# Attention's value products: one-pass products on the whole array in place of 64-column fp32 pairs

## The chip, the cores and the metric

The program runs on one core of one Trainium2 chip. A core has a matrix engine (TensorE, PE in the profile; its weight loads are PEld), an elementwise engine (VectorE, DVE), an engine for functions and copies (ScalarE, ACT), a general one (GpSimd, POOL) and an engine that issues transfers (SyncE, SP). TensorE writes to PSUM, which has eight banks of 128 partitions by 512 fp32 numbers; the others compute from there or from SBUF. The metric is the device time of one execution in microseconds. Before the change the median of three runs is 1974.89 us (1970.23 to 1979.09).

## The reference

Two layers of a block that mixes three token mixers over 1024 latent tokens (a grid of 16 rows and 64 columns) and 256 context tokens, width 1024, all in fp32. The input projection feeds neighbourhood attention (8 heads of 64), an mLSTM in two directions, and a Hyena long convolution; their gated outputs are concatenated, projected and added to the input. The part that matters here is the attention: a latent query sees keys in a window of 8 rows and 16 columns around it, with a bias by relative position, and all 256 context keys:

```python
s = jnp.concatenate([s_lat.reshape(s_lat.shape[:4] + (kr * NA_KBLK,)), s_ctx], axis=-1)
p = jax.nn.softmax(s, axis=-1).astype(v.dtype)
p_lat = p[..., :kr * NA_KBLK].reshape(s_lat.shape)
p_ctx = p[..., kr * NA_KBLK:]
o = jnp.einsum('bhjqic,bijchd->bjqhd', p_lat, vw) + jnp.einsum('bhjqn,bnhd->bjqhd', p_ctx, vc)
```

In the first layer the context tokens attend too, to the context alone. The last line, probabilities times values, is what the change rewrites.

## The kernel before

**Streams and the order of TensorE's work.** The kernel is written as Python generators, called streams, that emit instructions. TensorE's instructions run in the order in which they are emitted. Before TensorE work a stream yields what it needs (tiles, a free PSUM bank, or a name that another stream announces), and `flow` (line 196) picks the stream of the best rank whose needs are met by an estimated clock (`Clock`, line 48). That clock counts a TensorE product by `mm` (line 179), 70 ns and 1/960 us per element for a VectorE instruction, 80 ns and 1/1200 us for a ScalarE one (`RATE`, line 50), places each in its engine's first gap, and adds a margin of 0.3 us. Attention's units have rank 1, the preparation of keys and values 0.9, the input projections 2: projections fill what attention leaves. The order on the other engines is not written out by hand.

**Precision.** Two kinds of product occur. Where both operands are fp32, TensorE takes four passes over the columns, and a product leaves two rows in the trace. Where the operands are of the type `F32R`, it takes one pass and leaves one row; such an operand is split into a high part (rounded to that type) and a low part (what is left of the fp32 number), and products of the parts are summed. The projections and the scores are made so already: three products for a projection, two for the scores.

**Attention** (`na`, line 1246). For each layer and head, `keys` (line 1256) loads and splits queries and keys, and `values` (line 1280) loads the values of the context and of four column blocks, transposes them (tile `avt`) and copies them, tokens on partitions, to `aVn`, with 64 columns for the head. Four streams `work` (line 1311) take the units in turn: a unit is a head and a block of 16 grid columns, 256 queries in two halves of 128 (or, in layer 0, the 256 context queries). There are 40 units in layer 0 and 32 in layer 1. A unit

- makes the scores in PSUM (`apl` for the window, `apc` for the context), adds the bias on VectorE with the maximum, takes exponentials on ScalarE, and scales each row on GpSimd or VectorE (tile `ae`);
- then goes through up to three groups (line 1380): transposes the blocks of a group on TensorE into one of two `tp` banks (`apt`), copies them to SBUF (`ph`, ScalarE for groups 0 and 2, VectorE for group 1, line 1390), and in the next round multiplies them with the values (`apo`, line 1412). Groups 0 and 1 have 4 blocks, so two products of 256 columns, group 2 has 2 blocks, so two products of 128 columns; a context unit has group 0 alone;
- adds the two halves of the one output bank (`o`): ScalarE copies one half (`at`), VectorE adds the other (`ay`, line 1424), and the bank is free for the next unit.

The two products of a group have 64 columns of weights each, and go to the two halves of the array:

```python
for i, (t, s, os) in enumerate(groups[gi - 1][1]):
    self.mm(po[HP[i], os], lhsT=v[:, t, :], rhs=x[:, s], start=gi == 1, stop=gi == ng, beside=i > 0)
```

So the upper 64 rows of the output hold one key tile's part and the lower 64 the other's, and their sum is the result. Units keep their order by announced names (`pv`): the transposes of a unit's first group wait for the second group's products of the unit before, and its own first products for the last of that unit. `out_early` (line 1452) can start the output projection while heads are left, if the input projections are through by then.

Of the kernel before, what the change touches and what calls it, by code (L numbers as in the profile page):

```python
# [13 lines left out]
F32 = mybir.dt.float32  # L14
F32R = mybir.dt.float32r
BF16 = mybir.dt.bfloat16
ACTF = mybir.ActivationFunctionType
ALU = mybir.AluOpType
AX = mybir.AxisListType
PSUM = bass.MemoryType.PSUM  # L20
DRAM = bass.MemoryType.DRAM

DM = 1024          # model width
L, LC = 1024, 256  # latent and context tokens
LT = L + LC
NH = 256           # hyena channels
GW = 64            # grid width
# [3 lines left out]
NCH = LT // 128    # mLSTM chunks; 8 and 9 are the context  # L31

# column blocks of w_in, 128 columns each, in the order of the host layout
# [4 lines left out]
GM = 34            # the 16 gate columns, kept apart  # L38
# [3 lines left out]
RAWX, RAWC, RAWN = 1, 1027, 1284   # padded layout of the inputs of the short convolutions  # L42
UC = 1026                          # where the context starts in their outputs

BANKS = dict(pj=2, s=3, tp=2, o=1)  # uses of the PSUM banks


class Clock:
    """An estimate of when the emitted instructions run; the order of the tensor engine's follows it."""
    RATE = dict(vector=(0.07, 1 / 960), scalar=(0.08, 1 / 1200), gpsimd=(0.2, 1 / 480))   # us per instruction, per element  # L50
# [6 lines left out]
    def region(ap):  # L57
        """(tensor, rows, columns) that hold what an access pattern covers."""
# [13 lines left out]
    def ready(self, aps):  # L72
        """When all that is in aps is there."""
# [8 lines left out]
    def slot(self, ap):  # L82
        """When the memory of a tile is free of what was there before."""
# [15 lines left out]
    def vacant(self, key, bufs):  # L99
        """When the first of the memories of a kind is free."""  # L100
        taken = self.slots.get(key, [])
        return 0.0 if len(taken) < bufs else min(self.used.get(n, 0.0) for n in taken)

    def run(self, engine, us, after):
        """Put an instruction in the engine's first gap."""
# [40 lines left out]
class Timed:  # L146
    """An engine whose instructions the clock notes."""
# [13 lines left out]
class Kern:  # L161
    def __init__(self, tc, I, out, depth=2):
# [4 lines left out]
        self.fb = dict(o="o", s="s", tp="tp")     # banks of the filters  # L167
        self.known, self.streams, self.bankkey = set(), [], {}

    # ------------------------------------------------------------------ order of the tensor engine's work  # L170
    # Streams are generators that emit instructions. Before work of the tensor engine they yield what it needs, a
    # tuple of access patterns, or a time, or the name of something that another stream announces (a set: the first of them). The tensor
    # engine issues in the order of emission; of the streams that are ready by the clock, the first goes next.
# [5 lines left out]
    def mm(self, o, lhsT, rhs, start, stop, beside=False):  # L179
        """A matrix product; beside: on columns of the array next to those of the one before, at the same time."""  # L180
# [39 lines left out]
    # ------------------------------------------------------------------ set-up  # L220
# [19 lines left out]
    def want(self, tag, *aps, extra=0.0):  # L240
        """Wait until aps are there and a bank is free."""
# [8 lines left out]
    # columns of per-channel parameters: cols[:, l, ...]  # L250
# [4 lines left out]
    def small(self):  # L255
        """Small things that are needed all along."""
# [6 lines left out]
    # ------------------------------------------------------------------ adaLN  # L263
# [11 lines left out]
    def ada_mod(self, l, pool, ahead):  # L275
        """Shift and scale of a layer as columns."""
# [19 lines left out]
    def ada_cols(self, l, m, ks):  # L296
        """Columns ks of shift and scale from m, whose rows 32 q, 32 q + 1 hold the q-th quarter of them."""
# [17 lines left out]
    def ada_late(self, pool):  # L315
        """What is left of adaLN: the layers' gates and the second's shift and scale, in passing."""
# [4 lines left out]
        for j, (l, part, kt) in enumerate(todo):  # L321
# [26 lines left out]
            # the gate times the gain of the layer's last norm, as rows in DRAM  # L348
# [1642 lines left out]
```

## Time and profile before

| | |
|---|---|
| median of three runs | 1974.89 us |
| span of the profiled execution | 1971.5 us, 28340 instructions |
| TensorE busy | 1859.0 us (94%), 10008 products and transposes |
| VectorE busy | 1063.8 us (54%) |
| ScalarE busy | 787.1 us (40%) |
| GpSimd busy | 460.1 us (23%) |
| transfers | 328.91 MB, two hardware queues |

No other time of the profiled execution is recorded than its span; it lies 3.4 us below the median. A row of the profile names the line, engine and operation, the tiles (output, then inputs), and shapes as partitions by elements. Almost all instructions are emitted through helpers, so their line is that of a helper (L182 products, L186 transposes, L155 the rest) and the tiles tell them apart. Ends of TensorE's instructions are modelled and overlap the next one's start; the distance between starts is what an instruction costs the queue.

### The profile page before, as it was taken

To read this page: it belongs to the slowest core of one execution; us is meant where nothing else is said; L and a number is where in the kernel's file an instruction comes from. 1 tells how busy PE (TensorE), PEld (TensorE's weight loads), DVE (VectorE), ACT (ScalarE), POOL (GpSimd) and SP (SyncE) were. 2 spreads that over 40 slices of the span, in tenths; PEclk is the share of its full clock that TensorE was granted. 3 is DMA by queue.
4 is the path that set the end of the run, shared out by engine and by line. 5 is a ranking of instruction groups with operands and counts; after the bars stand their busy time and mean duration, and the time that the engine had idled before them with its cause. 6 is when DMAs were issued, how large, how long until landed. Compare 5 with 4: busy or idle time off the path is not lost. (4 is left out here: it accounts for less than half of the span.)

```text
span 1971.5 us, 28340 instructions
## 1 busy us (share of the span) xinstructions
PE 1859.0 (94%) x10008; PEld 1410.4 (72%) x10008; DVE 1063.8 (54%) x2398; ACT 787.1 (40%) x1545; POOL 460.1 (23%) x368
## 2 busy tenths in 40 slices
PE   8699989998999899999999999999799989999998
PEld 2365867787787776676777876778687867676776
DVE  3744444537736466676545544434753476666533
ACT  3645342414423255444434434322323255454321
POOL 1534111323220121121222123222412112122300
PEclk9799999999999999999999999999999999999999
DMA  8476887863221657666354348764221455454533
GB/s 316 140 239 212 284 232 241 235 229 104 81 82 46 180 146 224 194 212 216 105 192 139 139 146 234 224 196 162 80 96 65 141 150 160 129 157 134 180 128 107
DMA packets 233610, 328.91 MB, mean 167 GB/s; under 512 B 22509, under 2 KB 162185, under 8 KB 231550
## 3 DMA queue, kind: packets, MB, share of 16 engines
q1 hardware_dynamic: 186942, 264.45, 44.2%
q10 hardware_dynamic: 46528, 62.67, 9.0%
q8 instruction: 79, 1.29, 0.3%
q14 instruction: 61, 0.50, 0.1%
HBM read 230.82 MB, written 96.21 MB: 166 GB/s over the span
## 5 line engine op out<-in xcount | busy, mean ns | idle before, releaser
L182 PE MATMUL pj<-hhi,wh 128*128 128x512 f32 (+2 forms) x1504 | 599.4, 399 | 4.2 <-ACT sv L155 4.2
L182 PE MATMUL pj<-hlo,wh 128*128 128x512 f32 (+2 forms) x1504 | 552.6, 368 | 0.1
L182 PE MATMUL pj<-hhi,wl 128*128 128x512 f32 (+1 forms) x1456 | 535.3, 368 | 0.0
L182 PEld LDWEIGHTS pj<-hhi,wh 128*128 128x128 f32 (+1 forms) x1504 | 283.6, 189 | 73.7 <-issue 29.1
L182 PEld LDWEIGHTS pj<-hlo,wh 128*128 128x128 f32 (+1 forms) x1504 | 283.4, 188 | 48.7 <-issue 9.2
L182 PEld LDWEIGHTS pj<-hhi,wl 128*128 128x128 f32 x1456 | 275.7, 189 | 50.0
L155 POOL TENSOR_TENSOR wl<-wr,wh 128x1024 fp32r<-128x1024 f32 x68 | 163.5, 2404 | 541.1 <-ACT wh L155 505.6
L155 POOL TENSOR_SCALAR ae<-ae,ast 128x640 f32<-128x640 f32 (+1 forms) x72 | 69.4, 964 | 415.0 <-DVE ast L155 333.4
L155 ACT ACTIVATE ae<-ae,ast 128x640 f32<-128x640 f32 (+1 forms) x144 | 113.1, 787 | 106.8 <-DVE ast L155 102.6
L182 PE MATMUL op<-woh,yh 128*128 128x512 f32 x288 | 115.1, 400 | 9.1 <-ACT yh L155 9.1
L182 PE MATMUL apo<-ph,aVn 128*64 128x256 f32 (+1 forms) x800 | 113.8, 369 | 4.1 <-DVE ph L155 1.6
L182 PE MATMUL op<-woh,yl 128*128 128x512 f32 x288 | 114.7, 398 | 1.1 <-DVE yl L155 1.1
L182 PE MATMUL op<-wol,yh 128*128 128x512 f32 x288 | 113.9, 395 | 0.0
L155 ACT CAST wh<-wr 128x1024 fp32r<-128x1024 f32 (+1 forms) x70 | 72.0, 1028 | 101.2 <-PE pj L182 88.2
L155 ACT COPY ph<-apt 128x512 f32<-128x512 f32 (+1 forms) x136 | 65.6, 483 | 113.5 <-PE apt L186 110.4
L186 PE MATMUL apt<-ident,ae 128*128 128x128 f32 x672 | 109.1, 281 | 0.4 <-DVE ph L155 0.3
L186 PEld LDWEIGHTS apt<-ident,ae 128*128 128x128 f32 x672 | 76.9, 141 | 35.9 <-issue 24.7
L155 ACT COPY sr<-pj 128x512 f32<-128x512 f32 (+3 forms) x94 | 49.3, 525 | 132.5 <-PE pj L182 131.3
L155 DVE CUSTOM_DVE_ANT_0 ae<-apl,ab 128x384 f32<-128x384 f32 x128 | 69.5, 552 | 55.8 <-PE apl L182 32.8
L182 PEld LDWEIGHTS apo<-ph,aVn 128*64 128x64 f32 x800 | 40.8, 135 | 54.3 <-issue 28.4
L182 PEld LDWEIGHTS op<-woh,yh 128*128 128x128 f32 x288 | 55.5, 193 | 21.2 <-ACT yh L155 10.0
L155 POOL TENSOR_TENSOR zs<-zs,k 128x512 f32<-128x512 f32 x32 | 43.4, 1365 | 95.3 <-ACT zs L155 81.0
(255 smaller groups left out, 3040.5 us busy)
## 6 DMA issues: line engine op xcount, KB each, us to landing
wr<-in_wblk SPq DMA_DIRECT2D x68, 512.0 KB
wada<-in_wada SPq DMA_DIRECT2D x48, 512.0 KB
ab<-in_nab SPq DMA_DIRECT2D x96, 192.0 KB
pr<-sr ACTq DMA_DIRECT2D x64, 256.0 KB
k<-ks SPq DMA_DIRECT2D x128, 128.0 KB
raw<-pr SPq DMA_DIRECT2D x20, 512.0 KB
ark<-pr SPq DMA_DIRECT2D x32, 320.0 KB
gr<-yp SPq DMA_DIRECT2D x18, 512.0 KB
```

The source lines that it names most:

```text
L155: r = emit(*args, **kw)
L182: self.nc.tensor.matmul(o, lhsT=lhsT, rhs=rhs, start=start, stop=stop)
L186: self.nc.tensor.transpose(out=out, in_=in_, identity=identity)
```

## The change

The values and the transposed probabilities are split into a high and a low part of type `F32R`. A value tile holds 128 columns, [high 64; low 64]; a probability tile holds two planes. Each key tile is multiplied once with the high and once with the low probabilities, by products of 128 columns of weights on the whole array in one pass. The upper and the lower 64 rows of the output now hold the products with the high and with the low values, and the same sum as before adds them. A group has four products in place of two. ScalarE makes each high part (a copy that rounds), VectorE each low part (the PSUM tile minus the high part). Comments are also removed, and a reserve in SBUF for dynamic DMA is set to 1024.

```diff
-                v = pool.tile([128, 2 * g, 64], F32, name=f"aVn{n}_{b % 5}", tag="aVc" if b < 0 else "aVb", bufs=2 if b < 0 else 8)
+                v = pool.tile([128, 2 * g, 128], F32R, name=f"aVn{n}_{b % 5}", tag="aVc" if b < 0 else "aVb", bufs=2 if b < 0 else 8)
...
-                nc.vector.tensor_copy(v, tp[:, 0:g * 128].rearrange("p (t d) -> p t d", d=64))
+                tv = tp[:, 0:g * 128].rearrange("p (t d) -> p t d", d=64)
+                nc.scalar.copy(v[:, :, 0:64], tv)
+                nc.vector.tensor_tensor(out=v[:, :, 64:128], in0=tv, in1=v[:, :, 0:64].bitcast(F32), op=ALU.subtract)
...
-                        x = pool.tile([128, 512], F32, name=f"ph{nme}_{gi}", tag="ph", bufs=3)
+                        x = pool.tile([128, 2, 512], F32R, name=f"ph{nme}_{gi}", tag="ph", bufs=3)
                         w = len(groups[gi][0]) * 128
-                        (nc.vector.tensor_copy if gi == 1 else nc.scalar.copy)(x[:, :w], tp[:, :w])
+                        nc.scalar.copy(x[:, 0, :w], tp[:, :w])
+                        nc.vector.tensor_tensor(out=x[:, 1, :w], in0=tp[:, :w], in1=x[:, 0, :w].bitcast(F32), op=ALU.subtract)
...
-                    for i, (t, s, os) in enumerate(groups[gi - 1][1]):
-                        self.mm(po[HP[i], os], lhsT=v[:, t, :], rhs=x[:, s], start=gi == 1, stop=gi == ng, beside=i > 0)
+                    todo = [(t, part, s, os) for part in range(2) for t, s, os in groups[gi - 1][1]]
+                    for i, (t, part, s, os) in enumerate(todo):
+                        self.mm(po[:, os], lhsT=v[:, t, :], rhs=x[:, part, s], start=gi == 1 and i == 0, stop=gi == ng and i == 3)
...
-    nc = bacc.Bacc("TRN2", target_bir_lowering=False, num_devices=1)
+    nc = bacc.Bacc("TRN2", target_bir_lowering=False, num_devices=1, dynamic_dma_scratch_size=1024)
```

## Rows read from the trace of the kernel before

**Rows 1.** Head of the page: span, then busy time, share of the span, instructions.

```profile
span 1971.5 us, 28340 instructions
...
PE 1859.0 (94%) x10008; PEld 1410.4 (72%) x10008; DVE 1063.8 (54%) x2398; ACT 787.1 (40%) x1545; POOL 460.1 (23%) x368
```

**Rows 2.** Windows, both attention stretches: length, busy per engine, clock, DMA share, GB/s.

```profile
687.00:985.00 298.00, 293.68 (x1979) 212.19 (x1977) 197.84 (x602) 144.71 (x313) 58.16 (x49) 1.00 0.61 184
1583.00:1842.00 259.00, 254.65 (x1517) 184.33 (x1517) 163.72 (x503) 126.71 (x266) 53.31 (x40) 0.99 0.47 139
```

**Rows 3.** Windows, projections' tile alone, after layer 1's attention: PE, PEld, DVE, ACT.

```profile
1842.00:1868.00 26.00, 26.00 (x112) 20.91 (x113) 0.69 (x1) 2.99 (x5) 1.00 0.69 246
```

**Rows 4.** Groups by form, value products: busy us, mean ns, idle before.

```profile
L182 PE MATMUL apo<-ph,aVn 128*64 128x256 f32 x544 | 88.7, 405 | 3.3 <-DVE ph L155 1.6 <-DVE ay L155 1.3 <-ACT ph L155 0.3
...
L182 PE MATMUL apo<-ph,aVn 128*64 128x128 f32 x256 | 27.4, 292 | 0.8 <-ACT ph L155 0.7
```

**Rows 5.** Timeline of TensorE, start and length in us: first run, a middle one, last.

```profile
695.29 0.65 PE L182 MATMUL apo<-ph,aVn 128*64 128x256 f32 x4
695.87 0.44 PE L186 MATMUL apt<-ident,ae 128*128 128x128 f32 x2
696.24 0.44 PE L182 MATMUL apo<-ph,aVn 128*64 128x256 f32 x2
...
852.32 0.38 PE L186 MATMUL avt<-ident,av 128*128 128x128 f32 x2
852.54 0.38 PE L186 MATMUL adat<-ident,mada 128*128 128x128 f32 x2
852.85 0.87 PE L182 MATMUL apo<-ph,aVn 128*64 128x256 f32 x8
...
1841.02 0.87 PE L182 MATMUL apo<-ph,aVn 128*64 128x256 f32 x8
1841.82 0.50 PE L182 MATMUL pj<-hhi,wh 128*128 128x512 f32 x1
```

**Rows 6.** Timeline of TensorE, a narrow run and the score products behind it.

```profile
862.46 0.44 PE L182 MATMUL apo<-ph,aVn 128*64 128x128 f32 x4
862.83 0.45 PE L182 MATMUL apl<-kh,qs 128*128 128x384 f32 x1
863.11 0.34 PE L182 MATMUL apl<-kl,qs 128*128 128x384 f32 x1
863.29 0.28 PE L182 MATMUL apc<-kh,qs 128*128 128x256 f32 x1
863.40 0.28 PE L182 MATMUL apc<-kl,qs 128*128 128x256 f32 x1
...
864.00 0.28 PE L182 MATMUL apc<-kl,qs 128*128 128x256 f32 x1
864.12 0.38 PE L186 MATMUL apt<-ident,ae 128*128 128x128 f32 x2
```

**Rows 7.** Groups by form: copies of probabilities (whole span), gates from PSUM (layer 0).

```profile
L155 DVE COPY ph<-apt 128x512 f32<-128x512 f32 x64 | 43.8, 684 | 14.2 <-PE apt L186 13.8
L155 ACT COPY ph<-apt 128x512 f32<-128x512 f32 x72 | 42.1, 585 | 47.8 <-PE apt L186 47.5
...
L155 DVE SCALAR_TENSOR_TENSOR sz<-sz,pj 128x512 f32<-128x512 f32 x10 | 6.8, 684 | 4.4 <-ACT sz L155 4.4
...
L155 DVE SCALAR_TENSOR_TENSOR sz<-sz,pj 128x256 f32<-128x256 f32 x5 | 2.1, 415 | 1.3 <-ACT sz L155 1.3
```

**Rows 8.** Timeline: transposes in layer 1 and their copy.

```profile
1710.30 0.66 PE L186 MATMUL apt<-ident,ae 128*128 128x128 f32 x4
...
1711.46 0.56 ACT L155 COPY ph<-apt 128x512 f32<-128x512 f32 x1
```

**Rows 9.** Windows, 25 us of layer 0, columns as in group 2.

```profile
875.00:900.00 25.00, 25.00 (x176) 17.18 (x176) 19.01 (x58) 12.88 (x28) 6.22 (x5) 1.00 0.61 189
```

**Rows 10.** VectorE's waits in 1583 to 1842 us: total, times, longest.

```profile
DVE ast L155 <- ACT ae L155: 30.5, 22, 2.2
```

## The prediction
> **What bounds the kernel now.** Read the head of the page first: TensorE is busy 1859 us of a span of 1971.5 us [rows 1]. A product's duration overlaps the next one's, so this only says that TensorE nearly always has something in flight. Next take the two stretches in which attention runs, 687 to 985 us (layer 0) and 1583 to 1842 us (layer 1), 557 us together: TensorE is covered for 548 us of them at a granted clock of 0.99 to 1.00, VectorE for 198 of 298 us (66%) and 164 of 259 us (63%), ScalarE for 145 and 127 us [rows 2]. So here TensorE is the bound, and a microsecond taken off its queue is a microsecond off the end, as long as the other engines still deliver in time. Behind the second stretch projections fill 26 us of TensorE without a gap [rows 3], behind the first one nearly as much. They are work that can be issued earlier, inside the stretch, when attention is late.
>
> **TensorE: what the products cost now.** Take distances between starts, not durations. There are 400 products in 200 groups; each fp32 product leaves two rows, so 800 rows: 544 with 256 columns (136 groups), 256 with 128 (64 groups) [rows 4]. Following TensorE's instructions from the first of these rows (695.29 us) to the last run (1841.02), I count 186 unbroken runs: 122 of one 256-wide group, 50 of one 128-wide group, 14 of one of each [rows 5]. A run has three prices:
> - Going in. Two transposes are followed by two others after 0.22 us (852.32 to 852.54), so 0.11 each, but the products start 0.31 us after the second two: 0.09 extra [rows 5].
> - Itself. 0.58 us for a 256-wide group (695.29 to 695.87) and 0.80 for both in a row (1841.02 to 1841.82) [rows 5]; 0.37 for a 128-wide one (862.46 to 862.83) [rows 6]. The second group of the pair adds only 0.22, so a bare 256-wide group is about 0.43, and some 0.15 of each run is not columns but leaving this shape.
> - The next instruction. A score product after a run takes 0.28 (862.83 to 863.11), its successor 0.18 [rows 6]: 0.10 extra. Two transposes after a run take 0.37 up to the next products (695.87 to 696.24), 0.06 more than 0.22 and the 0.09 of going in [rows 5]. Half the runs are followed by transposes: 0.08 on average.
>
> Sum: 122 x 0.75 + 50 x 0.56 + 14 x 0.97 = 91.5 + 28.0 + 13.6 = 133.1 us.
>
> **TensorE: what they cost after.** 800 products, one row each, 128 columns of weights, no halves of the array. The nearest rows are the score products with the context, also one-pass, 128 by 128 with 256 columns: from one's start to the next instruction's it is 0.11 (863.29 to 863.40) and 0.12 us (864.00 to 864.12) [rows 6]. I take 0.116: 544 x 0.116 = 63.1 us. The second of these is followed by transposes and shows no extra, so the three prices above leave nothing behind. A one-pass product with 128 columns does not occur in the trace. Lower end 0.058, half of 0.116, if it follows its columns; upper end 0.22, the bare price of a 128-wide group now, if so narrow a product still runs in four passes: 14.8 to 56.3 us for 256 of them. I take the row with the same load and the same columns, the transpose at 0.11 [rows 5], rounded up to 0.113: 28.9 us. TensorE gains 133.1 - 63.1 - 28.9 = 41.1 us; with the ends, 55.2 and 13.7.
>
> The Trainium skill, "TensorE: Matmul & The Clock Gate", bears on this choice twice. Its section "LDWEIGHTS (loading the stationary operand)" has a load take its columns over 1.2 GHz, 107 ns for 128, which would hold the narrow products at 0.107 (an estimate: 27.4 us); its section "Back-to-back issue gap" puts an isolated gap at 56 ns for 128 columns (14.3 us). The gain would be 42.6 us by the first and 55.7 by the second. The transposes at 0.11 agree with the first.
>
> **VectorE and ScalarE: what is added.** Of the 200 transposed groups ScalarE now copies 72 wide ones (585 ns) and 64 half ones, VectorE 64 wide ones (684 ns) [rows 7]. After, ScalarE copies all and VectorE subtracts in all. A VectorE instruction of two inputs, one in PSUM, is not new: 684 ns for 512 columns and 415 for 256 in the gates [rows 7]. For the 64 groups that VectorE copied the price stays; for the rest it gains 72 x 0.684 + 64 x 0.415 = 49.2 + 26.6 = 75.8 us, 40.6 in layer 0 (40 wide, 32 half) and 35.2 in layer 1 (32 and 32). The values' 80 copies become subtractions of the same size. ScalarE gains 64 x 0.585 = 37.4 us and 80 copies of the values, below 0.585 each: it goes from 271 us to at most 356 of 557, which by itself hides. What may not hide is the order. A group is ready after 0.585 + 0.684 = 1.27 us in place of 0.6 or 0.7, and VectorE's subtraction now waits for ScalarE's copy, which queues behind exponentials: four transposes start at 1710.30, and their copy at 1711.46 [rows 8]. Behind that subtraction in VectorE's queue stand the reductions that free the score banks and the sums that free the one output bank, and TensorE waits for both.
>
> The larger tiles and the smaller reserve for dynamic DMA I cost at nothing: no transfer is added or moved in the program.
>
> **How much is given back.** VectorE's work becomes 197.8 + 40.6 = 238.4 us and 163.7 + 35.2 = 198.9 us, 437.3 together. If all of TensorE's 41.1 us arrived, the stretches would be 516 us and VectorE busy 85% of them, against 65% now. In the fullest 25 us in which TensorE had no gap it shows 19.0 us, 76% [rows 9], so that much is possible. Above about 88% it is not: waits for ScalarE's exponentials stand between VectorE's own instructions, 30.5 of 259 us in layer 1 [rows 10]. I take the middle, 82%: 238.4 / 0.82 = 290.7 and 198.9 / 0.82 = 242.6 us, 7.3 and 16.4 us less than now. Forecast: -23.7 us. Outside the two stretches nothing changes. The profiled execution's span is 1971.5 us, 3.4 below the median of 1974.9; counted from the median, 1951 us. With 80% and 84.5% for the 82% the gain is 10 and 39 us: the forecast's own range is 1936 to 1965.
>
> **Rivals.**
> - All of it arrives (1934 us): projections are pulled forward into attention whenever VectorE is late, so TensorE has no gap. For it: the 26 us of projections [rows 3] and an order of work that issues what it holds to be ready. Against: that order counts a VectorE instruction at 70 ns and 1/960 us per element (line 50), 603 ns for 512, below the 684 of [rows 7], so it will count on results too early.
> - The narrow products run in four passes: the gain is 13.7 us, VectorE at 80% is no longer the limit: 1961 us, and up to 10 more where waits add to it. No row of a narrow one-pass product speaks for or against it.
> - Slower: VectorE, with its queue blocked by ScalarE, gets no fuller than the 76% already seen. Then the stretches last 437.3 / 0.76 = 575 us, 18 more than now: 1993 us. It decides below 78.5% (437.3 / 557). For it: the chain of copy, subtraction and products passes through two queues that already wait for each other [rows 8, 10]. Against: the 76% was reached with TensorE full, so there VectorE also had to wait for TensorE, which is ahead when its products are shorter.
> - It does nothing (1975 us): TensorE's gain and new waits cancel, VectorE at about 78%.
>
> **How the numbers follow.** Forecast 0.45, all arrives 0.13, four passes 0.15, slower 0.20, nothing 0.07. 0.5% is 9.9 us, about what a measurement of this kernel (1970 to 1979 us in three runs) can tell from no change. Faster by more: 0.37 of the first, 0.13, and half of the third: 0.57. Slower by more: 0.17 of the fourth. The rest, 0.26, is the same. The range leaves out half of the second case and the larger half of the fourth: 1932 to 1986 us.
>
> **What would show it.** Right: the products' rows drop the half-array form, follow each other at 0.11 to 0.12 us whether 256 or 128 wide, and the instruction behind them pays no extra; attention's stretches are some 10 us shorter each with VectorE above 80%, and TensorE's waits name the probabilities' subtraction on VectorE. Wrong: narrow products 0.2 us apart; or stretches of the same length or longer with gaps in TensorE behind VectorE or ScalarE; or no gaps and the full 41 us.

## The result and the profile after

The change makes the kernel slower: 1988.25 us (median of 7 runs, 1984.09 to 1994.88) against 1973.27 before on the same chip, ratio 1.0058, 95% interval 1.0038 to 1.0078. The forecast was 1951, the range ended at 1986.

Head of the page of the changed kernel, columns as in [rows 1]:

```profile
span 1983.4 us, 28669 instructions
...
PE 1833.8 (92%) x10008; PEld 1476.2 (74%) x10008; DVE 1113.2 (56%) x2534; ACT 847.5 (43%) x1697; POOL 482.7 (24%) x376
```

Split each span into TensorE's busy time and the rest. Busy fell from 1859.0 to 1833.8 us (-25.2); the rest rose from 112.5 to 149.6 (+37.1). The difference of the two profiled spans, 11.9 us, is just that sum. Sum all waits of TensorE over the whole span by the engine that ended them: for VectorE they are 38.9 us before and 82.9 after, for ScalarE 43.1 and 29.1, for transfers 18.3 and 26.0. The largest rows after (us in total, times, longest):

```profile
PE apt L186 <- DVE aVn L155: 13.6, 11, 3.6
PE apo L182 <- DVE ay L155: 13.5, 9, 5.0
...
PE apt L186 <- DVE ph L155: 6.4, 4, 2.6
```

The value products by form, after, answering to [rows 4]:

```profile
L182 PE MATMUL apo<-ph,aVn 128*128 128x256 f32 x544 | 96.1, 299 | 16.4 <-DVE ay L155 13.5 <-DVE ph L155 1.7 <-ACT ph L155 1.0
...
L182 PE MATMUL apo<-ph,aVn 128*128 128x128 f32 x256 | 40.3, 277 | 2.2 <-DVE ph L155 1.8 <-ACT ph L155 0.3
```

One row for each product, whole array. A run of two groups beside scores on TensorE's timeline, answering to [rows 5, 6]:

```profile
860.48 1.03 PE L182 MATMUL apo<-ph,aVn 128*128 128x256 f32 x8
861.35 0.39 PE L182 MATMUL apl<-kh,qs 128*128 128x384 f32 x1
861.58 0.34 PE L182 MATMUL apl<-kl,qs 128*128 128x384 f32 x1
861.76 0.28 PE L182 MATMUL apc<-kh,qs 128*128 128x256 f32 x1
```

Eight products take 0.87 us, 0.11 each. The subtraction of the low part and the copy in front of it, by form, answering to [rows 7]:

```profile
L155 DVE TENSOR_TENSOR ph<-apt,ph 128x512 fp32r<-128x512 f32 x136 | 92.5, 685 | 32.8 <-ACT ph L155 32.3
L155 ACT CAST ph<-apt 128x512 fp32r<-128x512 f32 x136 | 78.2, 585 | 82.0 <-PE apt L186 79.2 <-DVE ast L155 1.2
...
L155 DVE TENSOR_TENSOR ph<-apt,ph 128x256 fp32r<-128x256 f32 x64 | 26.7, 417 | 13.3 <-ACT ph L155 13.2
```

Windows of both attention stretches after, from the first value product to the last, columns as in [rows 2]:

```profile
702.00:1049.00 347.00, 321.75 (x2167) 276.64 (x2165) 237.78 (x658) 185.02 (x398) 76.53 (x55) 0.99 0.56 174
1598.00:1897.00 299.00, 276.97 (x1652) 243.34 (x1651) 199.00 (x552) 165.44 (x343) 75.09 (x47) 0.97 0.46 140
```

The stretches are 646 us long. The windows of [rows 2] are not cut in the same way: both begin 8 us before the first value product of their layer, and the one of layer 0 ends 9 us before the last. From the first to the last value product the stretches were 298 and 250 us long before, 549 together, so they grew by 97 us. That is not the loss: projections that had stood behind attention [rows 3] moved into it (inside the stretches, counted from start to next start, projections rose from 258 to 293 us), and what follows each stretch up to the last output product fell from 151 to 103 and from 122 to 79 us. So a stretch's length says little about the time; the gaps do. Inside the stretches, so counted, they rose from 7.5 to 47.3 us.

What fills VectorE's queue tells more. Its waits in layer 0's stretch, before (687 to 985 us) and after (702 to 1049):

```profile
DVE ast L155 <- ACT ae L155: 18.0, 19, 1.9
DVE aVn L155 <- PE avt L186: 13.3, 11, 3.3
DVE ae L155 <- PE apl L182: 12.1, 13, 2.7
```

```profile
DVE ast L155 <- ACT ae L155: 33.7, 30, 1.9
DVE ph L155 <- ACT ph L155: 29.4, 26, 2.9
DVE aVn L155 <- ACT aVn L155: 8.2, 7, 2.6
DVE ae L155 <- PE apl L182: 7.0, 7, 1.7
```

Summed over all rows of both stretches VectorE waited 79.3 us for TensorE before and 15.5 after; for ScalarE 82.8 before and 174.4 after. Its own work and its waits for ScalarE are 361.6 + 82.8 = 444 of 557 us before (80%) and 436.8 + 174.4 = 611 of 646 after (95%). VectorE looks two thirds busy, but after the change most of its waits are for ScalarE. In part this is a change of names. Before, VectorE read 64 of the groups and all the values from PSUM, and so waited for the transposes itself; now ScalarE's copy stands between, and the wait is put down to ScalarE. In 41 of the 174 us (11 of 83 before) ScalarE was itself idle behind TensorE. Without them the sum is 78% before and 88% after. The rows show that TensorE waits for VectorE more than before; that ScalarE and VectorE together set the pace of attention is a reading of them, and the experiments bear it out only in part.

### The profile page after: what moved, and what is told of

Its sections match the earlier page's. It is cut to its first block, busy times and chain, and to the rows that moved or that the text cites. A ratio compares the mean times of both kernels' runs of the same rounds, so it can differ in the third digit from the quotient of the medians.

```text
span 1983.4 us, 28669 instructions
## 1 busy us (share of the span) xinstructions
PE 1833.8 (92%) x10008; PEld 1476.2 (74%) x10008; DVE 1113.2 (56%) x2534; ACT 847.5 (43%) x1697; POOL 482.7 (24%) x376
## 5 line engine op out<-in xcount | busy, mean ns | idle before, releaser
L182 PE MATMUL pj<-hhi,wh 128*128 128x512 f32 (+2 forms) x1504 | 593.3, 395 | 4.3 <-ACT sv L155 4.3
L155 POOL TENSOR_SCALAR ae<-ae,ast 128x640 f32<-128x640 f32 (+1 forms) x72 | 75.3, 1046 | 437.2 <-DVE ast L155 392.0
L155 ACT CAST ph<-apt 128x512 fp32r<-128x512 f32 (+1 forms) x200 | 101.5, 517 | 116.8 <-PE apt L186 112.8
L182 PE MATMUL apo<-ph,aVn 128*128 128x256 f32 (+1 forms) x800 | 134.0, 292 | 18.6 <-DVE ay L155 13.5
L155 DVE TENSOR_TENSOR ph<-apt,ph 128x512 fp32r<-128x512 f32 (+1 forms) x200 | 119.0, 599 | 46.1 <-ACT ph L155 45.5
L182 PEld LDWEIGHTS apo<-ph,aVn 128*128 128x128 f32 x800 | 113.7, 194 | 34.7 <-DVE ay L155 16.3
L182 PE MATMUL op<-woh,yh 128*128 128x512 f32 x274 | 110.0, 401 | 0.3 <-DVE xr L155 0.3
L182 PE MATMUL op<-woh,yl 128*128 128x512 f32 x274 | 108.1, 395 | 0.9 <-DVE yl L155 0.9
L182 PE MATMUL op<-wol,yh 128*128 128x512 f32 x274 | 107.7, 393 | 0.0
L155 DVE CUSTOM_DVE_ANT_0 ae<-apl,ab 128x384 f32<-128x384 f32 x128 | 69.3, 551 | 23.5 <-PE apl L182 15.5
```

The source lines that it names most:

```text
L155: r = emit(*args, **kw)
L182: self.nc.tensor.matmul(o, lhsT=lhsT, rhs=rhs, start=start, stop=stop)
```

## The experiments

Three explanations stood against each other. **Chain:** a group of probabilities takes longer from transposes to products, since a subtraction follows the copy. **Load:** VectorE has 200 more instructions in its queue, and everything behind them is later. **Order:** the clock that orders TensorE's work misjudges the new costs, or other work is left uncovered. Unless said otherwise an edit is against the changed kernel, ratios are against the kernel before on the same chip, with 95% intervals; 0.001 is 2 us. e1, e3, e8, e11, e13 and e14 leave out the probabilities' low part, e4 and e12 make a low part of zero.

**The form alone** (e1): new products, no subtraction.

```diff
-nc.scalar.copy(x[:, 0, :w], tp[:, :w])
-nc.vector.tensor_tensor(out=x[:, 1, :w], in0=tp[:, :w], ... op=ALU.subtract)
+(nc.vector.tensor_copy if gi == 1 else nc.scalar.copy)(x[:, 0, :w], tp[:, :w])
...
-yield x, v, 0.5
+yield x[:, 0], v, 0.5
...
-... rhs=x[:, part, s] ...
+... rhs=x[:, 0, s] ...
```

> The new products alone: four whole-array one-pass products per group, but the probabilities have no low part (the high plane is multiplied twice, so the result is not the reference's), and the groups are copied as before, by ScalarE or, for group 1, by VectorE. Values are still split. Theory A (a unit's chain of copy and then subtraction sets attention's pace, so attention outlasts the projections and TensorE runs out of work): the chain is as short as before, TensorE's saving arrives: 1935 to 1950 us, attention ends before the projections in both layers. Theory B (the new product form is not cheaper, or the values' split costs the time): 1970 us or more. Theory C (VectorE has too much work): as A here, VectorE has less work.

1972.08 us, ratio 0.9984 (0.9961 to 1.0006): no change that can be told. TensorE's busy time fell by 19 us, to 1840.0, but the rest of the span rose to 136.2. Of the 24 us of gaps that were added 15 stand inside the stretches and 10 behind them (2 fewer elsewhere). The largest new wait is at the output projection, whose weights and last inputs were covered by projections before (16.0 us against 9.1).

**The chain alone** (e2), against the kernel before: its old products read a second plane that VectorE writes after ScalarE's copy. The smaller reserve for dynamic DMA is set too, as in the changed kernel.

```diff
-(nc.vector.tensor_copy if gi == 1 else nc.scalar.copy)(x[:, :w], tp[:, :w])
+nc.scalar.copy(x[:, 0, :w], tp[:, :w])
+nc.vector.tensor_tensor(out=x[:, 1, :w], in0=tp[:, :w], in1=x[:, 0, :w], op=ALU.max)
...
-... rhs=x[:, s] ...
+... rhs=x[:, 1, s] ...
```

> The chain alone, in the kernel before: fp32 pairs of 64 columns as before, but each transposed group goes through ScalarE's copy and then a VectorE instruction of the subtraction's size (the maximum of the bank and the copy, which is the same number), and the products read that. Theory A: the old price of the products plus the longer chain: 2000 to 2025 us, attention's stretches 340 us or more and 290 or more. Theory B (product form or values' split): 1970 to 1980 us. Theory C (VectorE's load): 1985 to 2010 us, with VectorE over 75% busy in the stretches.

2003.44 us, 1.0156 (1.0118 to 1.0194). The second step costs 31 us with the old products, and the stretches are as long as in the changed kernel (344 and 300 us). This does not separate chain from load.

**Parts of the chain.** e3 keeps the subtraction, but the products read and wait for the high part alone (the two edits of e1 at the yield and the operand):

> The changed kernel with VectorE's subtraction still made from the PSUM bank, but the products read the high plane twice and wait for ScalarE's copy alone (the result is not the reference's). VectorE's work and the time for which a transposed group's bank is held stay. Theory A1 (the products' wait for the subtraction is what lengthens the chain): 1940 to 1955 us. Theory A2 (the bank is held until the subtraction has read it, and the next transposes wait for a bank): 1980 to 1990 us. Theory C (VectorE's load): 1980 to 1990 us.

2013.83 us, 1.0205 (1.0168 to 1.0242). Stretches 311 and 285 us, shorter, and yet slower: a stream of adaLN weights was left over behind attention, and TensorE waited for its loads. Waits of TensorE in e3:

```profile
PE ada L182 <- DMA wada<-in_wada: 34.7, 18, 8.3
```

e4 frees the bank of the transposes after the copy: the subtraction takes `in0=x[:, 0, :w]` instead of `tp`, so its result is zero.

> The changed kernel with the subtraction's first input in SBUF (the high plane minus itself, so the low part is zero and the result is only as exact as the high part): the bank is free after ScalarE's copy, while products still wait for both planes and VectorE has as many instructions of the same size. Theory A1 (products' wait): 1980 to 1990 us. Theory A2 (bank held): 1940 to 1960 us. Theory C (VectorE's load): 1980 to 1990 us.

1983.49 us, 1.0041 (1.0020 to 1.0062); stretches 332 and 285. The interval overlaps the changed kernel's. e12 does the same for the values (`in0=v[:, :, 0:64]` instead of `tv`):

> The changed kernel with only the values' subtraction moved off its PSUM bank (it reads the high half in SBUF, so the values' low part is zero and the result only as exact as their high part). In the changed kernel transposes wait 14 us in all for a bank that the values' subtraction holds. If that hold matters for the time: 1973 to 1983 us, attention's stretches 10 us or more shorter each. If the probabilities' chain sets it: within 5 us of the changed kernel's 1988 us.

1991.47 us, 1.0078 (1.0058 to 1.0097): nothing gained. e5 issues the products of a group's high part at once and those of its low part one group later:

```diff
+emit(gi - 1, 0, v)
+if gi > 1:
+    emit(gi - 2, 1, vc if gi == 2 else vb)
+if gi == ng:
+    yield x[:, 1], 0.0
+    emit(gi - 1, 1, v)
```

> The changed kernel, whole computation, with the products in another order: a group's products with the high probabilities wait for ScalarE's copy alone and come first, those with the low ones follow a group later, when VectorE's subtraction is long done (for the last group of a unit at once). Theory A1 (the wait for the subtraction lengthens a unit's chain): attention's stretches 310 to 335 and 283 to 292 us, time 1970 to 1983 us. Theory A2 (the bank held by the subtraction is all of it): stretches as in the changed kernel (347 and 298), 1984 to 1992 us.

2034.88 us, 1.0294 (1.0247 to 1.0340). Attention and projections ended together in layer 1, and the output projection stood 23.0 us waiting.

e11 cuts the chain and keeps the load: e3 and e4 together. Nobody reads the subtraction and it holds no bank.

> The changed kernel with all of VectorE's subtractions for the probabilities still issued at their size, but on nobody's path: they read the high plane in SBUF (so the bank is free after ScalarE's copy) and the products read the high plane twice and wait for ScalarE alone (the low part is left out, the result is not the reference's). Theory A (the chain, its product wait and its bank hold, is what lengthens attention): stretches 290 to 305 and 250 to 262 us, as in the form alone, 1968 to 1985 us. Theory C (VectorE's 76 us of added work lengthen it by themselves): stretches 310 us or more and 275 or more, 1985 us or more.

1999.33 us, 1.0111 (1.0094 to 1.0128). Windows of its stretches:

```profile
697.00:985.00 288.00, 274.13 (x1918) 237.93 (x1917) 230.13 (x650) 170.69 (x379) 61.01 (x46) 0.99 0.58 177
1609.00:1868.00 259.00, 241.29 (x1507) 211.57 (x1506) 198.69 (x545) 149.87 (x325) 56.61 (x38) 0.99 0.46 136
```

Without the chain the stretches are 547 us, as in e1. But the time did not come back: 25 us above e1 by the ratios. e11 differs from e4 in one thing: the products do not wait for the subtraction. It is 14 us slower by the ratios, with stretches 71 us shorter; e3 likewise is 29 us slower than the changed kernel, with stretches 50 us shorter. So the wait of the products makes the stretches longer, and taking it away alone gave no time back.

**The order.** e6 hides the subtraction from the clock, so that the order is made without it (`self.tc.nc.vector` instead of `nc.vector`); e7 raises the clock's cost per instruction from 0.07 to 0.15 us (VectorE) and from 0.08 to 0.16 (ScalarE).

> The changed kernel, whole computation, but the clock by which TensorE's order is written does not count the probabilities' subtraction: the order is written as if products waited for ScalarE's copy alone. If the longer chain acts through the written order (attention's instructions are put late, projections in front of them), attention's stretches come down to 293 to 315 and 252 to 275 us and the time to 1970 to 1982 us. If it acts on the chip itself, TensorE stands in gaps behind VectorE: more than 50 us of gaps in the two stretches, 1985 to 2005 us.

> The changed kernel, whole computation, with the order's clock counting 150 ns in place of 70 for a VectorE instruction and 160 in place of 80 for a ScalarE one, as the trace has them. If TensorE's gaps inside attention (25 and 22 us) come from an order that expects results too early, they fall below 25 us together and the time to 1970 to 1980 us, with projections pulled forward and attention no shorter. If the chain on the chip sets the time: 1984 to 1995 us.

e6: 2001.56 us, 1.0149 (1.0107 to 1.0192); stretches 313 and 257 us, but 56 us of gaps in them. The wait is real, and the order that knows of it does better. e7: 2080.49 us, 1.0550 (1.0507 to 1.0593). It reorders the whole program, the parts before attention too (the first score comes 34 us later than in the kernel before), so it says nothing on the cause.

**What TensorE still gives.** e8 is e1 with half of the products (`range(1)` for `part`):

> As the new form alone (short chain, no low part of the probabilities), and each key tile is multiplied once in place of twice, so TensorE has 400 products in place of 800 and some 45 us less work (the result is not the reference's). Theory P (attention's units, not TensorE, set the pace of the stretches, and TensorE's free time becomes gaps): stretches 285 to 300 and 245 to 257 us, 1955 to 1972 us. Theory Q (TensorE's work sets the time): 1925 to 1938 us.

1954.34 us, 0.9899 (0.9862 to 0.9935). 400 products fewer took 48 us off TensorE's busy time against e1 (1791.9), and 17 of them arrived by the ratios. TensorE is still worth something, at well under one for one.

**The cover of w_out's load.** The output projection's weights are loaded twice, in the kernel before (e9) and in the changed one (e10):

```diff
 nc.sync.dma_start(out=raw[j], in_=self.I["wout"][l, order[j]])
+nc.sync.dma_start(out=raw[j], in_=self.I["wout"][l, order[j]])
```

> The kernel before, whole computation, with each tile of the output projection's weights loaded twice in a row (4.2 MB more in each layer, 10 to 20 us of transfers). Theory: in the kernel before, the 25 to 30 us of projections after attention's end just cover that load, so they are no slack; the second load stands open: 15 to 40 us slower, TensorE in gaps before the first output products. If they are slack (as the prediction took them): no more than 6 us.

> The changed kernel, whole computation, with the same second load. There projections end 50 to 70 us before attention, and the load lies beside attention's last units: within 6 us of the changed kernel's 1988 us (up to 10 if the transfers delay attention's own loads). If the load counts wherever it stands: 15 to 40 us slower, as in the kernel before.

e9: 1995.13 us, 1.0086 (1.0059 to 1.0114), 17 us dearer than without; e10: 1995.05, 1.0083 (1.0050 to 1.0115), 5 dearer by the ratios, with overlapping intervals. The kernel before has little slack there; the changed one, where projections end 50 to 70 us ahead of attention, has more.

**Load or chain, by additions and removals.** e13 is e1 with ScalarE copying all groups, as the changed kernel does; against the changed kernel it lacks the subtraction alone. e14 is e11 with the copies shared as in e1; against e1 it adds the unread subtraction alone.

> The form alone as before (the low part of the probabilities left out), but ScalarE copies all 200 groups, so the 64 wide middle groups move from VectorE (684 ns each) to ScalarE (585 ns): 44 us off VectorE, 37 us onto ScalarE. Theory S (what the load without the chain still cost, 27 us over the form alone, is ScalarE's queue: copies stand behind exponentials there): 1990 to 2002 us, TensorE's waits for ScalarE's copies (apo and apt behind ph on ACT) at 15 us or more. Theory V (it is VectorE's added subtractions, even though nothing waits for them): 1965 to 1977 us, since VectorE has less to do than in the form alone. Theory O (the order merely falls out otherwise, so that other streams are left over at the end): between, 1977 to 1990, with the loss outside the two stretches.

> The load without the chain (products read the high plane alone and wait only for it; the subtraction reads the high plane, holds no bank, and its result is read by none), but the middle group's copy is back on VectorE: only the subtractions are added to the form alone, 200 of them, 114 us of VectorE. Theory S: 1968 to 1982 us, waits behind ScalarE's copies back under 8 us. Theory V: 1990 to 2005 us, with waits behind VectorE (ph, aVn, ay) in place of those behind ScalarE. Theory O: 1980 to 1992.

e13: 1960.03 us, 0.9903 (0.9881 to 0.9925). e14: 2002.70 us, 1.0122 (1.0096 to 1.0148), stretches 320 and 285. ScalarE's copies are no cost here, they are a gain (that it comes from the 44 us of work that VectorE loses is not shown: the same edit of the kernel before, e16, is slower); VectorE's unread subtractions cost 27 us against e1. Nobody waits for them, and yet e14's stretches are 605 us long, so a chain is not needed for long stretches. Windows of e13 and of e14:

```profile
697.00:982.00 285.00, 270.38 (x1936) 234.24 (x1935) 170.83 (x546) 168.09 (x375) 56.95 (x46) 0.99 0.59 186
1588.00:1834.00 246.00, 229.40 (x1460) 205.26 (x1459) 141.22 (x449) 148.56 (x323) 49.87 (x37) 0.97 0.47 140
```

```profile
698.00:1018.00 320.00, 303.00 (x2101) 259.42 (x2100) 253.58 (x688) 156.74 (x354) 65.31 (x47) 0.99 0.55 170
1611.00:1896.00 285.00, 265.50 (x1612) 233.69 (x1611) 230.27 (x585) 147.97 (x309) 80.16 (x47) 0.97 0.47 145
```

VectorE is 59% busy in e13's stretches and 80% in e14's. In e14 it waits 7.9 us for TensorE in both stretches together. TensorE's longest wait stands behind attention, at the low part of w_out, which VectorE makes. This is mostly no delay by VectorE's queue: VectorE itself stood idle for 11.2 us in front of it, until the load of w_out had come. e17 (below) has the same. The rows of e14, then of e17:

```profile
PE op L182 <- DVE wol L155: 21.7, 1, 21.7
DVE wol L155 <- DMA wos<-in_wout: 11.2, 1, 11.2
...
PE op L182 <- DVE wol L155: 18.0, 1, 18.0
PE op L182 <- ACT yh L155: 16.8, 2, 13.5
DVE wol L155 <- DMA wos<-in_wout: 7.7, 1, 7.7
```

e15 puts copy and subtraction of the middle group into VectorE's one queue, with the whole computation (the copy's line as in e1, the rest as changed):

> The changed kernel, whole computation, with the middle group's copy on VectorE, so that copy and subtraction of 64 of the 200 groups follow each other in one queue; VectorE gains 44 us, ScalarE loses 37. If it is the hop between two queues that makes the chain long: 1970 to 1984 us, stretches under 335 and 288 us. If VectorE's load or the plain sum of the two durations (0.68 + 0.68 us in place of 0.59 + 0.68): 1988 to 2010 us, stretches as long as in the changed kernel (347 and 299 us) or longer.

1991.88 us, 1.0071 (1.0045 to 1.0098). No hop between queues for 64 of the groups, and nothing gained.

**The same in the old form.** e16 is the kernel before with all copies on ScalarE (one line). e17 is the kernel before with an unread VectorE instruction for every group (products read plane 0, the added instruction is a subtraction at the place of e2's, with `in0=x[:, 0, :w]`; the reserve is set as in e2). e18 is the changed kernel with the normalisation of each unit's second half on ScalarE:

```diff
+nc.vector.tensor_scalar(out=c(6), in0=c(5), scalar1=0.5, scalar2=None, op0=ALU.mult)
...
-(nc.vector if hf else nc.gpsimd).tensor_scalar(out=x, in0=x, scalar1=st[:, 5, hf:hf + 1], scalar2=0.5, ...)
+if hf:
+    nc.scalar.activation(out=x, in_=x, func=ACTF.Copy, scale=st[:, 6, 1:2])
+else:
+    nc.gpsimd.tensor_scalar(out=x, in0=x, scalar1=st[:, 5, 0:1], scalar2=0.5, ...)
```

> The kernel before, whole computation, with one line changed: ScalarE also copies the 64 middle groups that VectorE copied, so 44 us leave VectorE and 37 go to ScalarE; the products stay as they were. Load theory (what the attention stretches and their tails cost is set by how much stands in VectorE's queue, whatever waits for it): the same gain as with the new products, some 12 to 18 us: 1957 to 1965 us. Chain theory (what counts is how long a group of probabilities takes from transposes to products): the copy takes 585 in place of 684 ns but queues behind exponentials, so 1968 to 1980 us, no change that can be told.

> The kernel before, whole computation, with 200 VectorE instructions of two inputs added, one for each copied group, whose result is read by none: products read and wait for the copy alone, the added instruction reads the copy and holds no bank; 114 us at the rows' prices for operands in one bank. The old products then have what the load with shared copies had with the new ones (2003 us). Load theory: 25 to 35 us more than before, 2000 to 2012 us, as much as the chain with its load cost in the old form (2003), so that the chain's own part is small. Chain theory: work that nobody waits for hides beside TensorE: 1970 to 1985 us.

> The changed kernel, whole computation, with another piece of VectorE's work given to ScalarE: the normalisation of every unit's second half (72 instructions of 579 to 591 ns, some 40 us), against one short VectorE instruction per unit (72 of about 0.2 us, 14 us): 26 us off VectorE, some 45 us onto ScalarE. Load theory: 8 to 12 us less than the changed kernel, 1974 to 1981 us. Chain theory: the chain from exponentials to transposes gets one step longer (0.2 us and a hop to ScalarE's queue), so 1988 to 2000 us.

e17: 2025.44 us, 1.0255 (1.0228 to 1.0282): 50 us for work that nobody waits for, more than load and chain together cost in e2 (31). But e17 adds 139 us to VectorE where e2, whose copies moved to ScalarE, adds 76, and most of its new gaps are at the output projection (the rows above), not in attention. e18: 1981.03 us, 1.0028 (1.0006 to 1.0049), 6 us under the changed kernel with a longer chain; the direction is that of the load, but the intervals overlap. e16: 1986.28 us, 1.0063 (1.0041 to 1.0085), slower, which both explanations missed. Its stretches are shorter than before's (280 and 240 us), but the projections left over behind them are longer, and they ran into the split of their own weights on ScalarE. TensorE's waits in e16:

```profile
PE pj L182 <- ACT wh L155: 10.4, 2, 6.1
```

**All pairs.** Each row has the same copies and the same VectorE work for the probabilities, each column the same products and the same handling of the values (new products go with split values). The reserve for dynamic DMA is the smaller one in all but the kernel before and e16; no run changes it alone:

| copies and added VectorE work | old products | new products | new against old | TensorE busy, old and new (us) |
|---|---|---|---|---|
| shared, none | before 1 | e1 0.9984 | -3 us | 1859.0, 1840.0 |
| all on ScalarE, none | e16 1.0063 | e13 0.9903 | -32 us | 1862.6, 1837.0 |
| all on ScalarE, second step waited for | e2 1.0156 | changed 1.0058 | -19 us | 1864.8, 1833.8 |
| shared, unread step | e17 1.0255 | e14 1.0122 | -26 us | 1873.5, 1837.7 |

The differences are those of the ratios times 1975 us. With the VectorE work held equal the new products are worth 19 to 32 us in three of four pairs. Down the columns, VectorE's second step costs 31 us from e13 to the changed kernel, 18 from e16 to e2, 50 and 27 unread. With all copies on ScalarE an unread step cost 41 us (e13 to e11).

Where TensorE's gaps stand in the profiled executions (one of each kernel; us; "in" is from the first to the last value product of both layers, "behind" from there to the layer's last output product; the rest of the span has 91 to 99 us of gaps in each):

| kernel | in | behind |
|---|---|---|
| before | 7.5 | 10.4 |
| e16 | 10.7 | 16.9 |
| e2 | 31.0 | 5.4 |
| e17 | 19.3 | 35.9 |
| e1 | 22.6 | 20.8 |
| e13 | 31.2 | 6.2 |
| changed | 47.3 | 3.2 |
| e14 | 36.5 | 25.8 |
| e11 | 31.6 | 25.5 |

Two things can be read here. In all four pairs the new products bring 15 to 21 us of gaps into the stretches (7.5 to 22.6, 10.7 to 31.2, 31.0 to 47.3, 19.3 to 36.5), so a good part of what TensorE saves is given back there, with or without the subtraction. And a second step that is waited for adds its gaps in the stretches (20 from e16 to e2, 16 from e13 to the changed kernel), while an unread one adds 0 to 14 there and 5 to 26 behind them, at the output projection.

## Why the prediction was wrong

- **"TensorE gains 41.1 us": right in kind, too large.** The side of before was right: its 186 runs take 101.0 us from start to next start, and with the prices of going in and out (0.09 and 0.08 for each run) 132.6, against 133.1 forecast (its 0.56 for a narrow run should be 0.54 by its own prices, 1 us). After, the products take some 105 us by the same count (gaps left out) instead of 92.0: 0.53 us for a group where 0.46 was forecast. Some 7 us of that belong to the transposes in front of 92 of the runs, the last of which starts 0.03 us ahead of the run in place of 0.11. The narrow ones run in one pass, 0.112 us apart (median between starts) against 0.113 forecast, neither bound came true, and projections that follow a run pay no extra (0.23 us, 0.34 before). The busy time fell by 25.2. Of the two rules of the Trainium skill, "TensorE: Matmul & The Clock Gate", the trace agrees with "LDWEIGHTS (loading the stationary operand)" and its 107 ns for 128 columns, with 112 ns measured. The 56 ns of "Back-to-back issue gap" are not what narrow products take behind each other; the section itself calls them an isolated gap, and its 81 ns for a stream of loads and products are below the 112 too.
- **"A microsecond taken off its queue is a microsecond off the end, as long as the other engines still deliver in time": its condition did not hold.** In three of the four pairs 26, 31 and 36 us less busy time gave 32, 19 and 26; from the kernel before to e1, 19 gave 3. In all four 15 to 21 us of new gaps in the stretches stand against the saving, and what the pair was worth in the end depended on the gaps behind the stretches. What is special about the first pair was not settled; of e1's 24 us of added gaps 15 stand in the stretches, and 7 are ScalarE's part of the wait at the output projection's start.
- **VectorE's added work: right.** 238.4 and 198.9 us were forecast for the two stretches, 237.8 and 199.0 came. The fit is closer than the reasoning deserves, since the stretches after are longer and hold other work of VectorE as well; the price of a subtraction (0.684 and 0.415 us forecast, 0.685 and 0.417 measured) was right.
- **"Above about 88% it is not [possible] ... I take the middle, 82%": the step that failed.** VectorE was busy 69% and 67% of the stretches. The 12% of waiting that stood behind the 88% was read from the one row of [rows 10], in a kernel in which the copies did not yet stand in front of VectorE's work. The change itself adds waits of the same kind: 200 subtractions and 80 of the values each wait for a copy on ScalarE, and with the reductions that wait for exponentials VectorE stood waiting for ScalarE 27% of the stretches (174.4 of 646 us) instead of 15%. The text named this wait [rows 8] and then gave it no price. Own work and waits for ScalarE make 95% of the stretches, 88% without the waits in which ScalarE stood behind TensorE. That sum is a sign and no measure: it is 97% in e11, whose stretches are as short as e1's (89%). With it fell the other half of the step, "Outside the two stretches nothing changes": the stretches grew by 97 us where 24 less were forecast, and what stands behind them shrank by 91.
- **The slower rival** (1993 us, VectorE no fuller than 76%) named the mechanism and the side, and came within 5 us. Its price was right by chance: it put the loss into the stretches' length, and they grew by 97 us (89 over the windows of [rows 2]), not 18; most of this came back behind them as projections already done. The loss is 37 us of gaps in TensorE (40 more in the stretches), 44 more behind VectorE and some less behind others, against 25 us of work saved. By the runs some 15 of the 40 came with the new products (e1), 9 with the copies' move to ScalarE (e1 to e13) and 16 with the subtraction (e13 to the changed kernel).
- **"They are work that can be issued earlier": right,** 35 us of projections moved forward. They fill waits; once they have run out, at 978 us of 1049, nothing does. The windows after that point in layer 0, and in layer 1, where they end at 1845:

```profile
978.00:1049.00 71.00, 58.03 (x400) 47.56 (x398) 47.36 (x127) 40.25 (x83) 24.96 (x15) 0.95 0.60 199
...
1845.00:1897.00 52.00, 38.98 (x219) 34.41 (x218) 31.51 (x77) 30.99 (x58) 22.89 (x12) 0.84 0.42 137
```

TensorE's gaps are 13 of 71 and 13 of 52 us there, 26 of the 47 us of gaps in both stretches. The signs listed under "Wrong", longer stretches with gaps behind VectorE, are the ones that came.

**Still open.** That the subtraction turned the gain into a loss is shown: without it, and with nothing else changed but the plane that the products read, the kernel is 31 us faster (e13) and beats the kernel before by 19. How it costs this was not separated. Its own time in VectorE's queue, the time for which the queue stands still in front of it, and the products' wait for it all remain: the unread subtraction of e11, e14 and e17 also follows ScalarE's copy, it is longer (below), and much of its cost came where w_out's load was not covered. The smaller reserve for dynamic DMA and the larger tiles, which the prediction put at nothing, were not tested by themselves. And the order reacts to every edit: e3, e5 and e16 lost time to a stream left uncovered, not to what they were made to test. No version with the whole computation beat the kernel before; e13 and e8 did, without the probabilities' low part.

## What to carry to other kernels

An engine that is full because work of low rank fills it is not shown to be the bound: here the change took 25 us off TensorE's work and brought 40 us of gaps into stretches that TensorE had filled. Look at whom the others wait for. An engine that is two thirds busy may have little room left if its other waits are for the partner with which it alternates, so price those waits before taking a limit for its share, and follow each one on: a wait for the partner can be a wait for the first engine under another name. A split into high and low parts saves on the matrix engine and is paid on the elementwise one: here 119 us of subtractions on VectorE (in place of 44 us of copies) for 25 us of TensorE. And where an order is planned, test each half of a change on top of both versions of the other half: the same products were worth 3 us in one setting and 32 in another. Then see where the gaps stand, since an edit in one stage can be paid at the start of the next.

## What the hardware showed that was not expected

The same subtraction is slower from SBUF than from PSUM while GpSimd works. In e11 both operands lie in SBUF. Its rows by form:

```profile
L155 DVE TENSOR_TENSOR ph<-ph 128x512 fp32r<-128x512 f32 x136 | 106.0, 780 | 20.6 <-ACT ph L155 20.3
...
L155 DVE TENSOR_TENSOR ph<-ph 128x256 fp32r<-128x256 f32 x64 | 32.5, 507 | 4.8 <-ACT ph L155 4.5
```

780 and 507 ns against 685 and 417 with one operand in PSUM. The excess lies where GpSimd is busy at the same time: of the 200, the 64 that overlap a GpSimd instruction take 851 ns on average and up to 2568, the other 136 take 619 and at most 695. In the changed kernel, with `tp` as an operand, the 62 that overlap (both widths, as above) take 563 and at most 692. So e4, e11, e14 and e17, whose added instruction reads SBUF alone, carry 138 to 150 us of subtraction where the changed kernel carries 119. The Trainium skill states the like in "SBUF — State Buffer", section "Who interferes with whom": a VectorE instruction with two SBUF inputs contends with a GpSimd instruction that reads SBUF. The trace agrees, and shows the size.
